# Values' stage of a one-core diffusion backbone: own buffers for the modulations' weights, TensorE's order by hand, fillers

## The chip, the cores and the metric

The kernel runs on one core of a Trainium2 chip. The metric is the time of one execution on the device in microseconds (us), from the first instruction to the last; lower is better. The kernel before took 1047.04 us, the median of 3 runs (1046.14 to 1047.27).

## The reference, cut to what matters

Two token groups go through two layers: 128 prompt tokens and 256 sample tokens, model width 1024. Each layer is a token mixer and a gated feed-forward, each after an RMSNorm and a modulation. What the change touches is the beginning of layer 0:

```python
sm, cm, gm, sf, cf, gf = adaln(c_ctx or c, w_ada[l], b_ada[l])  # silu(cond) @ w_ada + b_ada, split in 6
h = rmsnorm(x, g) * (1 + cm) + sm
q, k, v = qkv_proj(h, w_qkv)                # 1024 -> 3 * 1024
mix = attention(q, k, v) @ w_attn_out       # 16 heads of 64, with a position bias from rpb
```

So the values, v = h @ w_v, need h, and h needs 1/rms of every token and the shift sm and scale cm of every feature. Those come from a product of the two conditioning vectors (one for the prompt, one for the samples) with the first 2048 columns of w_ada.

## The kernel before, in words

Activations lie with features on partitions: x is eight tiles of 128 features by 384 tokens. All products are in float32 made of two parts: every operand is split into a high and a low part (hi and lo), and a product is three matmuls (hi by hi, hi by lo, lo by hi; the helper `mac`, L102 to L105). ScalarE (ACT) makes the high part of a weight tile (L96), VectorE (DVE) the low part (L97); `load` (L88) does both for a unit of 4 KB per partition, from a staging pool `stg` of three buffers into pools of five.

The values' stage, in the first lines of `attention` (L396 to L418), goes like this. `square` makes the squares of x, on ScalarE, and VectorE adds them up (L266 to L271); TensorE (PE) sums them over the partitions (`sums`, L280). `ada_block(0)` makes shift and scale of feature tile 0: 16 matmuls with 32-column stationary tiles (L145), ScalarE copies the result to SBUF (`ada_sb`, L149), TensorE transposes it (L151), and three small VectorE instructions (L154, L157, L117) finish the modulations `mod`. Then 1/rms is spread over the partitions by three matmuls (L294) and ScalarE copies it to SBUF (`R`, L404). For each feature tile k of eight: `modulated` makes h (VectorE's `t` L320, ScalarE's `hhi` L322, VectorE's `hlo` L324); the weights w_v of tile k are loaded; `ada_block(k + 1)` is written; and 18 matmuls of 512 columns add tile k's share to six PSUM banks (three token blocks by two halves of the features). At the end ScalarE copies the six banks to `V` (L417).

Then come, per pair of heads, `keys` and `queries` (24 matmuls each from a unit of w_qk, L103 to L105; their splits `ks` L440 and L441, `qd` and `ql` L453 to L455), `bias` (four DMAs into the one buffer `btr`, L471, and one VectorE instruction that writes `bt`, L477) and `scores` (L462 and L463, then VectorE's maxima L500 that read `bt`).

Two things set the order. A framework places each engine's instructions in one fixed order when the kernel is built, by priorities and its own estimate, except where `tc.keep_in_program_order` pins them; each engine then works through its list in that order. And a buffer of a pool is written again only when its last reader is done: `adp`, with ADA_BUFS = 4 buffers, holds the weights of two `ada_block`s (two tiles each, 512 KB a tile), which SyncE's queue (SP) issues in line with all other loads. `ps_ad`, with one PSUM bank, takes the sums of one `ada_block`.

Of the kernel before, what the change touches and what calls it, by code (L numbers as in the profile page):

```python
# [8 lines left out]
F32 = mybir.dt.float32  # L9
# [23 lines left out]
# columns of the packed per-feature parameters  # L33
# [6 lines left out]
def backbone(ctx: ExitStack, tc: tile.TileContext, xT_in, cond_in, condr_in, b_ada_in, prm_in,  # L40
# [21 lines left out]
    cond = cst.tile([P, KD, 2], F32, name="cond")  # L62
    nc.gpsimd.dma_start(cond, cond_in)
    x = [cst.tile([P, NT], F32, name=f"x{k}") for k in range(KD)]
    for k in range(KD):
        nc.sync.dma_start(x[k], xT_in[:, k, :])
# [10 lines left out]
    # TensorE runs at half its clock until it has been busy for a while  # L77
# [23 lines left out]
    def mac(out, a, b, start, stop):  # L101
        """out (+)= a.T @ b, both as (hi, lo)"""  # L102
        nc.tensor.matmul(out, a[0], b[0], start=start, stop=False)  # L103
        nc.tensor.matmul(out, a[0], b[1], start=False, stop=False)  # L104
        nc.tensor.matmul(out, a[1], b[0], start=False, stop=stop)  # L105
# [16 lines left out]
    def ada_load(f):  # L122
        w = []
        for hf in range(2):
            st = adp.tile([P, D], F32, name="adw", tag="adw")
# [4 lines left out]
    w_first = ada_load(0)  # L130
# [5 lines left out]
    def ada_block(f, tpool=ps_tb):  # L136
# [3 lines left out]
        w = ada_load(f) if f else w_first  # L140
        for kk in range(4):
            for hf in range(2):
                for q in range(2):
                    j = 2 * hf + q
                    nc.tensor.matmul(pa[32 * j:32 * j + 32, 0:P], cond_s[:, 4 * hf + kk, :],  # L145
                                     w[hf][:, kk, P * q:P * q + P], start=(kk == 0),
                                     stop=(kk == 3), tile_position=(0, 32 * j))
# [12 lines left out]
    class Ada:  # L160
        """pieces of 1024 modulations on TensorE, one unit (a feature tile of the conditioning)
        at a time; units are loaded ahead of their products"""
# [35 lines left out]
        def flush(self):  # L198
            """[32j + conditioning, 256 columns] to features on partitions"""
# [18 lines left out]
    class AdaV:  # L218
        """modulations on VectorE, 128 at a time"""
# [55 lines left out]
    def sums(pin=False):  # L275
        """every token's sum of squares"""
# [9 lines left out]
    def rms(ss=None, pin=False):  # L286
        """1/rms of every token, on all partitions: [P, NT] in PSUM"""
# [12 lines left out]
    def rsqrt(src, v, scale):  # L300
        """(src * scale + EPS) ** -0.5, refined by one Newton step"""
# [11 lines left out]
    # the modulated input of a layer's first products; its last two columns are the shifts  # L313
# [26 lines left out]
    def norm_first(nxt, units):  # L340
        """the first tiles' products as the tiles of x come, then h; returns the banks and R"""
# [13 lines left out]
    def late(ps, R, wkp):  # L355
        """products with 1/rms, and the shifts' products to add to them"""
# [23 lines left out]
    def attention(pool, wkp):  # L380
        # 0 where key column cc is in the window of query column c, else NEG
# [10 lines left out]
        V = pool.tile([P, 3, D], F32, name="V")  # L392
# [3 lines left out]

        # V, all its tiles at once, as the tiles of h come
        for k in range(KD):
            square(k, ("t384", "t384", "R0")[k % 3])
        ss = sums(True)  # L400
        ada_block(0, ps_ta)
        Rp = rms(ss, True)
        R = tmp.tile([P, NT], F32, name="R0", tag="R0")
        nc.scalar.copy(R, Rp[:, :NT])  # L404
        acc = [bank(q) for q in (ps_mm, ps_mm, ps_mm, ps_sc, ps_sc, ps_ta)]
        for k in range(KD):
# [391 lines left out]
```

## Time and profile before

| what | value |
|---|---|
| runs | 1047.27, 1047.04, 1046.14 us |
| span of the profiled execution | 1046.2 us |
| TensorE busy | 1027.7 us, 98% of the span |
| VectorE, ScalarE, GpSimd busy | 796.9, 496.8, 13.3 us |
| DMA | 174.32 MB, mean 167 GB/s |
| TensorE busy, 0 to 20 us | 13.91 us, granted clock 0.81 |
| TensorE busy, 20 to 66 us | 46.00 us, granted clock 0.97 |

The profile is of one execution, 0.8 us under the median of the runs. A row of the timeline reads: start, duration, engine, line, operation, what it writes and reads, count, and in brackets how long the engine stood before it and what released it. fp32 matmuls show as two records each. PEld is TensorE's loading of stationary tiles. In the rows of windows the columns are the stretch, its length, then busy time (and records) of the engines, the granted clock of TensorE, the DMA engines' busy share, and GB/s.

### The profile page before, as it was taken

What the parts mean: (1) busy time and instruction counts of PE and PEld (TensorE: products, weight loads), DVE (VectorE), ACT (ScalarE), POOL (GpSimd) and SP (SyncE); (2) the same over time, 40 slices, a digit from 0 to 9 for tenths busy, and PEclk for the clock granted to TensorE, in tenths of its full rate; (3) what the DMA queues carried; (4) which work ended last, traced back from release to release, by engine and by line L of the source; (5) the groups of instructions that cost most, each with busy time, mean ns of one, the idle gap of its engine ahead of it and who ended that gap; (6) DMA issues with size and microseconds to landing.
All of it is one profiled execution on the core that took longest, in us unless ns stands there. A gap on an engine that the chain in (4) does not pass through costs nothing.

```text
span 1046.2 us, 16013 instructions
## 1 busy us (share of the span) xinstructions
PE 1027.7 (98%) x5964; PEld 959.3 (92%) x5964; DVE 796.9 (76%) x1697; ACT 496.8 (47%) x862; POOL 13.3 (1%) x27
## 2 busy tenths in 40 slices
PE   7999999999999999999999999999999999999996
PEld 6787777679999999999998889999999999999995
DVE  3557666628899898999989979888599777777653
ACT  3357566536765544433346344444375544453330
POOL 1000000000000000000000000000000000000000
PEclk8999999999999999999999999999999999999998
DMA  7867666515255454566665765665414434435521
GB/s 274 310 191 208 187 186 194 192 61 171 81 153 181 161 156 150 161 199 211 217 196 174 247 205 157 198 191 195 144 65 157 142 122 123 134 109 169 163 69 61
DMA packets 64717, 174.32 MB, mean 167 GB/s; under 512 B 18800, under 2 KB 24064, under 8 KB 64640
## 3 DMA queue, kind: packets, MB, share of 16 engines
q1 hardware_dynamic: 63632, 171.46, 52.1%
q8 instruction: 47, 0.77, 0.3%
q0 software_dynamic: 432, 1.06, 0.3%
q10 hardware_dynamic: 576, 0.79, 0.2%
q14 instruction: 30, 0.25, 0.1%
HBM read 170.66 MB, written 2.62 MB: 166 GB/s over the span
## 4 chain that ended last, share of the span: by engine, by line
PE 92%; DMA 3%; DVE 2%; ACT 1%; SPq 1%; issue 1%; POOL 0%; POOLq 0%; DVEq 0%
PE bank L103 27%; PE bank L105 27%; PE bank L104 27%; DMA btr<-in_rpb 2%; PE bank L535 2%; PE bank L463 1%; PE bank L462 1%; PE bank L687 1%; PE bank L190 1%; PE bank L145 1%; PE bank L524 1%; DMA adw<-in_w_ada 1%; PE bank L532 1%; SPq L471 1%; PE bank L294 1%
## 5 line engine op out<-in xcount | busy, mean ns | idle before, releaser
L96 ACT CAST hi<-st 128x1024 fp32r<-128x1024 f32 (+1 forms) x216 | 222.5, 1032 | 315.3 <-PE bank L104 260.3
L105 PE MATMUL bank<-hhi,lo 128*128 128x384 f32 (+1 forms) x960 | 325.6, 339 | 0.4 <-DVE lo L97 0.4
L103 PE MATMUL bank<-hhi,hi 128*128 128x384 f32 (+1 forms) x960 | 325.7, 339 | 0.0
L104 PE MATMUL bank<-hlo,hi 128*128 128x384 f32 (+1 forms) x960 | 325.1, 339 | 0.0
L97 DVE TENSOR_TENSOR lo<-st,hi 128x1024 fp32r<-128x1024 f32 (+1 forms) x216 | 259.7, 1203 | 80.7 <-ACT hi L96 80.3
L103 PEld LDWEIGHTS bank<-hhi,hi 128*128 128x128 f32 x960 | 181.2, 189 | 3.5 <-issue 3.0
L105 PEld LDWEIGHTS bank<-hhi,lo 128*128 128x128 f32 x960 | 181.2, 189 | 1.3 <-DVE lo L97 0.7
L104 PEld LDWEIGHTS bank<-hlo,hi 128*128 128x128 f32 x960 | 180.6, 188 | 0.1
L248 DVE CUSTOM_DVE_ANT_0 junk<-adw,cs 128x1024 bf16<-128x1024 f32 x112 | 136.7, 1220 | 1.0
L105 PE MATMUL bank<-ahi,lo 128*128 128x384 f32 x352 | 119.0, 338 | 0.0
L104 PE MATMUL bank<-alo,hi 128*128 128x384 f32 x352 | 119.0, 338 | 0.0
L103 PE MATMUL bank<-ahi,hi 128*128 128x384 f32 x352 | 118.8, 338 | 0.0
L105 PEld LDWEIGHTS bank<-ahi,lo 128*128 128x128 f32 x352 | 66.1, 188 | 0.0
L104 PEld LDWEIGHTS bank<-alo,hi 128*128 128x128 f32 x352 | 66.1, 188 | 0.0
L103 PEld LDWEIGHTS bank<-ahi,hi 128*128 128x128 f32 x352 | 66.1, 188 | 0.0
L103 PE MATMUL bank<-hi,hhi 128*128 128x512 f32 x144 | 58.3, 409 | 1.8 <-ACT hhi L322 1.8
L105 PE MATMUL bank<-hi,hlo 128*128 128x512 f32 x144 | 57.5, 399 | 0.0
L104 PE MATMUL bank<-lo,hhi 128*128 128x512 f32 x144 | 57.4, 399 | 0.0
L368 DVE SCALAR_TENSOR_TENSOR x<-bank,mod,x 128x128 f32<-128x128 f32 x64 | 23.9, 413 | 37.6 <-PE bank L105 37.6
L103 PE MATMUL bank<-mhi,hi 128*128 128x384 f32 x128 | 43.4, 339 | 0.0
L105 PE MATMUL bank<-mhi,lo 128*128 128x384 f32 x128 | 43.2, 338 | 0.0
L104 PE MATMUL bank<-mlo,hi 128*128 128x384 f32 x128 | 43.1, 337 | 0.0
(151 smaller groups left out, 1288.7 us busy)
## 6 DMA issues: line engine op xcount, KB each, us to landing
st<-in_w_up SPq DMA_DIRECT2D x88, 512.0 KB, 3.5
adw<-in_w_adaT SPq DMA_DIRECT2D x56, 512.0 KB, 3.6
adw<-in_w_ada SPq DMA_DIRECT2D x40, 512.0 KB, 5.8
st<-in_w_down SPq DMA_DIRECT2D x32, 512.0 KB, 3.6
st<-in_w_qk SPq DMA_DIRECT2D x16, 512.0 KB, 6.7
st<-in_w_gu SPq DMA_DIRECT2D x16, 512.0 KB, 4.2
st<-in_w_gv SPq DMA_DIRECT2D x16, 512.0 KB, 4.3
st<-in_w_gout SPq DMA_DIRECT2D x16, 512.0 KB, 4.2
```

Of the source, the lines that this page charges most:

```text
L96: nc.scalar.copy(hi[:, :n], st[:, :n])
L97: nc.vector.tensor_tensor(lo[:, :n], st[:, :n], hi[:, :n].bitcast(F32), ALU.subtract)
L103: nc.tensor.matmul(out, a[0], b[0], start=start, stop=False)
L104: nc.tensor.matmul(out, a[0], b[1], start=False, stop=False)
L105: nc.tensor.matmul(out, a[1], b[0], start=False, stop=stop)
L145: nc.tensor.matmul(pa[32 * j:32 * j + 32, 0:P], cond_s[:, 4 * hf + kk, :], w[hf][:, kk, P * q:P * q + P], start=(kk == 0), stop=(kk == 3), ...
L190: nc.tensor.matmul(self.pa[32 * j:32 * j + 32, 0:256], cond_s[:, k, :], t[:, 256 * j:256 * j + 256], start=(k == 0), stop=(k == KD - 1), t ...
L248: tc.keep_in_program_order(nc.vector.tensor_tensor_reduce(self.junk, t, self.cs[c], 1.0, 0.0, ALU.mult, ALU.add, m[:, c:c + 1]))
L294: mm = nc.tensor.matmul(R[:, b * P:(b + 1) * P], r[:, b:b + 1].to_broadcast([P, P]), ident, start=True, stop=True)
L368: nc.vector.scalar_tensor_tensor(x[m][:, a:b], ps[:, a:b], mod(l, gate, m, c), x[m][:, a:b], ALU.mult, ALU.add)
L462: nc.tensor.matmul(out, qd[hh][:, qs], ks[hh][:, cs], start=True, stop=False)
L535: nc.tensor.matmul(pv[hs, NPR:NT], vv, pT[:, 256 * i:256 * i + 256], start=(i == 0), stop=(i == 2), tile_position=(0, 64 * hh))
```

## The change

Beside comments, it does the following.

- x is loaded in four DMAs of two tiles each, where there were eight.
- The values' stage is a function of its own, `project_values`, and V lies in a pool `v` around it. Inside, a pool `vw` of six buffers takes the weights of `ada_block(1)` to `ada_block(7)`; `ada_block(0)` still uses `adp`. The attention's pools `att` and `attw` are opened after `vw` is closed, so their first tiles (the mask, `cv`, the attention's results) lie where `vw` was.
- The loads for blocks 1 and 2 are issued right after w_v's first tile; those for block k + 3 in step k, after w_v's tile k + 1.
- The 16 matmuls of each `ada_block` and the values' matmuls are pinned in the order they are written: 18 matmuls of tile k, by part (six hi by hi, six with h's low part, six with w's low part), then `ada_block(k + 2)`; after tile 0, blocks 1 and 2. The transposes are not pinned.
- Fillers: five matmuls of 128 columns after the sums of squares, and six after those that spread 1/rms.
- Tile 0's `t` reads 1/rms from PSUM; the copy to SBUF serves the other tiles.

```diff
+    xp = [cst.tile([P, 2, NT], F32, name=f"x{k}") for k in range(0, KD, 2)]
+    x = [xp[k // 2][:, k % 2, :] for k in range(KD)]
+    for k in range(KD // 2):
+        nc.sync.dma_start(xp[k], xT_in[:, 2 * k:2 * k + 2, :])
...
+    def project_values(V, vp):
...
+        def keep_warm(src, n):
+            warm = bank(ps_ad)
+            for _ in range(n):
+                tc.keep_in_program_order(
+                    nc.tensor.matmul(warm[:, :P], src[:, :P], ones, start=True, stop=True))
+
+        aw = {0: w_first}
+        ws = {0: load(w_v[0])}
+        for f in (1, 2):
+            aw[f] = ada_load(f, vp)
+        for k in range(KD):
+            square(k, ("t384", "t384", "R0")[k % 3])
+        ss = sums(True)
+        keep_warm(sq["last"], 5)
+        ada_block(0, aw.pop(0), ps_ta)
+        Rp = rms(ss, True)
+        keep_warm(ones, 6)
...
+        for k in range(KD):
+            modulated(0, SM, CM, k, R if k else Rp)
+            if k == 0:
+                nc.scalar.copy(R, Rp[:, :NT])
+            if k + 1 < KD:
+                ws[k + 1] = load(w_v[k + 1])
+            if k + 3 < KD:
+                aw[k + 3] = ada_load(k + 3, vp)
+            w = ws.pop(k)
+            for part, (ih, iw) in enumerate(((0, 0), (1, 0), (0, 1))):
+                for half in range(2):
+                    for b in range(3):
+                        tc.keep_in_program_order(nc.tensor.matmul(
+                            acc[3 * half + b], h(k, slice(b * P, (b + 1) * P))[ih],
+                            w[iw][:, half, :], start=(k == 0 and part == 0),
+                            stop=(k == KD - 1 and part == 2)))
+            for f in (k + 2,) if k else (1, 2):
+                if f in aw:
+                    ada_block(f, aw.pop(f))
...
-        for k in range(KD):
-            modulated(0, SM, CM, k, R)
-            w = load(w_v[k])
-            if k < KD - 1:
-                ada_block(k + 1)
-            for half in range(2):
-                for b in range(3):
-                    mac(acc[3 * half + b], h(k, slice(b * P, (b + 1) * P)),
-                        wsel(w, half, slice(0, 512)), k == 0, k == KD - 1)
```

What this does to the built order shows in three places. First TensorE, in the middle of the stage, where one `ada_block` (`adw`) and its transpose (`ada_sb`) stand among the values' matmuls (`hhi` and `hlo` are h, `hi` and `lo` the weights). Before:

```order
L105 MATMUL bank<-hi,hlo 128x512
L145 MATMUL bank<-adw,cond_s 32x128 x16
L103 MATMUL bank<-hi,hhi 128x512
L104 MATMUL bank<-lo,hhi 128x512
L105 MATMUL bank<-hi,hlo 128x512
L151 MATMUL bank<-ident,ada_sb 128x128
L103 MATMUL bank<-hi,hhi 128x512
```

And now, the same place:

```order
L415 MATMUL bank<-lo,hhi 128x512 x6
L146 MATMUL bank<-adw,cond_s 32x128 x16
L152 MATMUL bank<-ident,ada_sb 128x128
L415 MATMUL bank<-hi,hhi 128x512 x6
L415 MATMUL bank<-hi,hlo 128x512 x6
```

The transpose stood two to six values' matmuls behind the block whose result it takes; now it follows it directly, with ScalarE's copy between the two.

Second VectorE, at the passage from the last tile of h (`hlo`) to the first scores; `bt` is a pair's bias, `ks` and `ql` the low parts of keys and queries, the ISA rows the scores' maxima. Before:

```order
L324 SCALAR_TENSOR_TENSOR hlo<-t_680,mod_143,hhi 128x256
L97 TENSOR_TENSOR lo<-st,hi 128x1024 x2
L477 TENSOR_TENSOR bt<-btr,mask 128x768
L97 TENSOR_TENSOR lo<-st,hi 128x1024 x2
L441 TENSOR_TENSOR ks<-kT,ks 64x512 x2
L477 TENSOR_TENSOR bt<-btr,mask 128x768
L455 SCALAR_TENSOR_TENSOR ql<-bank,qd 64x384
L500 ISA bank,st<-bank,bt 128x256
```

And now:

```order
L325 SCALAR_TENSOR_TENSOR hlo<-t_660,mod_135,hhi 128x256
L500 TENSOR_TENSOR bt<-btr,mask 128x768
L98 TENSOR_TENSOR lo<-st,hi 128x1024 x2
L500 TENSOR_TENSOR bt<-btr,mask 128x768
L464 TENSOR_TENSOR ks<-kT,ks 64x512 x2
L478 SCALAR_TENSOR_TENSOR ql<-bank,qd 64x384 x2
L523 ISA bank,st<-bank,bt 128x256
```

The bias of the second pair moved from behind the first keys' low parts to ahead of them.

Third SyncE's queue, at the end of the stage. Before:

```order
L93 DMA st<-in_w_v 128x1024
L420 DMA cv<-in_cv 128x1024
L430 DMA kT<-in_ckT 128x128
L93 DMA st<-in_w_qk 128x1024 x2
L471 DMA btr<-in_rpb 64x6x64 x4
L430 DMA kT<-in_ckT 128x128
```

And now:

```order
L94 DMA st<-in_w_v 128x1024 x2
L453 DMA kT<-in_ckT 128x128
L94 DMA st<-in_w_qk 128x1024
L494 DMA btr<-in_rpb 64x6x64
L94 DMA st<-in_w_qk 128x1024
L494 DMA btr<-in_rpb 64x6x64 x2
L443 DMA cv<-in_cv 128x1024
L494 DMA btr<-in_rpb 64x6x64
L453 DMA kT<-in_ckT 128x128
L94 DMA st<-in_w_qk 128x1024 x2
```

`cv` moved behind three of the four bias loads, and it waits for the last matmuls of `ada_block(7)`, whose buffers it lies in.

More of the change, by code (lines that the diff above doesn't have):

```diff
@@ L63, in backbone @@
     nc.gpsimd.dma_start(cond, cond_in)
-    x = [cst.tile([P, NT], F32, name=f"x{k}") for k in range(KD)]
-    for k in range(KD):
-        nc.sync.dma_start(x[k], xT_in[:, k, :])
+    xp = [cst.tile([P, 2, NT], F32, name=f"x{k}") for k in range(0, KD, 2)]
+    x = [xp[k // 2][:, k % 2, :] for k in range(KD)]
+    for k in range(KD // 2):
+        nc.sync.dma_start(xp[k], xT_in[:, 2 * k:2 * k + 2, :])
     zero = cst.tile([P, 1], F32, name="zero")
@@ L120, in gain, with ada_load @@
             ALU.add, ALU.mult)
-    def ada_load(f):
+    def ada_load(f, pool):
         w = []
         for hf in range(2):
-            st = adp.tile([P, D], F32, name="adw", tag="adw")
+            st = pool.tile([P, D], F32, name="adw", tag="adw")
             w.append(st.rearrange("p (a b) -> p a b", b=256))
@@ L144, in ada_block @@
                     j = 2 * hf + q
-                    nc.tensor.matmul(pa[32 * j:32 * j + 32, 0:P], cond_s[:, 4 * hf + kk, :],
-                                     w[hf][:, kk, P * q:P * q + P], start=(kk == 0),
-                                     stop=(kk == 3), tile_position=(0, 32 * j))
+                    tc.keep_in_program_order(
+                        nc.tensor.matmul(pa[32 * j:32 * j + 32, 0:P], cond_s[:, 4 * hf + kk, :],
+                                         w[hf][:, kk, P * q:P * q + P], start=(kk == 0),
+                                         stop=(kk == 3), tile_position=(0, 32 * j)))
         sb = tmp.tile([P, 256], F32, name="ada_sb", tag="ada_sb")
@@ L377, in wsel, with attention @@
         return w[0][:, k, s], w[1][:, k, s]
-    def attention(pool, wkp):
+    def project_values(V, vp):
+        def keep_warm(src, n):
+            warm = bank(ps_ad)
+            for _ in range(n):
+                tc.keep_in_program_order(
+                    nc.tensor.matmul(warm[:, :P], src[:, :P], ones, start=True, stop=True))
[10 more added lines that the diff above has]
+        keep_warm(ones, 6)
+        R = tmp.tile([P, NT], F32, name="R0", tag="R0")
+        acc = [bank(q) for q in (ps_mm, ps_mm, ps_mm, ps_sc, ps_sc, ps_ta)]
+        for k in range(KD):
[17 more added lines that the diff above has]
+                    ada_block(f, aw.pop(f))
+        for b in range(3):
+            for half in range(2):
+                nc.scalar.copy(V[:, b, 512 * half:512 * half + 512], acc[3 * half + b])
+        nc.gpsimd.dma_start(sv_out, V[:, 0, :])
+    def attention(V, pool, wkp):
         mask = pool.tile([P, 64], F32, name="mask")
@@ L395, in attention @@
         olo = [pool.tile([P, NT], F32R, name=f"olo{t}") for t in range(NPAIR)]
[L398 to L406, printed above, removed]
-            modulated(0, SM, CM, k, R)
-            w = load(w_v[k])
-            if k < KD - 1:
-                ada_block(k + 1)
-            for half in range(2):
-                for b in range(3):
-                    mac(acc[3 * half + b], h(k, slice(b * P, (b + 1) * P)),
-                        wsel(w, half, slice(0, 512)), k == 0, k == KD - 1)
-        for b in range(3):
-            for half in range(2):
-                nc.scalar.copy(V[:, b, 512 * half:512 * half + 512], acc[3 * half + b])
-        nc.gpsimd.dma_start(sv_out, V[:, 0, :])
         nc.sync.dma_start(cv, cv_in)
@@ L710, in gmlp @@
             residual(1, GM, m, ps, (1, SF, CF))
-    with tc.tile_pool(name="att", bufs=1) as pool, tc.tile_pool(name="attw", bufs=2) as wkp:
-        attention(pool, wkp)
+    with tc.tile_pool(name="v", bufs=1) as vpool:
+        V = vpool.tile([P, 3, D], F32, name="V")
+        with tc.tile_pool(name="vw", bufs=6) as wkp:
+            project_values(V, wkp)
+        with tc.tile_pool(name="att", bufs=1) as pool, tc.tile_pool(name="attw", bufs=2) as wkp:
+            attention(V, pool, wkp)
     csp = ctx.enter_context(tc.tile_pool(name="cs", bufs=1))
```

6 lines of the change are left out of this document (2 added, 4 removed).

## Prediction, made before the change was run

> **What bounds the kernel now.** I read the page first, then who TensorE waits for, then the timeline of the first 80 us.
>
> ```profile
> span 1046.2 us, 16013 instructions
> ...
> PE   7999999999999999999999999999999999999996
> ```
> ```profile
> PE bank L294 <- DVE rr L310: 1.9, 1, 1.9
> PE bank L103 <- ACT hhi L322: 1.8, 1, 1.8
> PE bank L280 <- DVE sqacc L271: 1.8, 1, 1.8
> ...
> PE bank L145 <- DMA adw<-in_w_ada: 0.7, 1, 0.7
> ```
>
> TensorE is busy from the first slices to the last: whatever delays it by 1 us anywhere makes the kernel 1 us longer. Only the first slice has room. And the modulations' weights (`adw`), which now get six buffers, hold TensorE up once, 0.7 us, for the block that keeps its old buffers. So loading ahead brings nothing by itself; the order does whatever is done. The stage to be costed ends where the first keys begin:
>
> ```profile
> 3.27 0.52 ACT L266 ACTIVATE sqacc<-x 128x384 f32<-128x384 f32 x1 [1.03 <-DMA x<-in_xT]
> 4.91 0.22 ACT L72 ACTIVATE cond_s<-cond 128x16 f32<-128x16 f32 x1 [1.12 <-DMA cond<-in_cond]
> 5.57 3.88 DVE L271 TENSOR_TENSOR sqacc<-sqacc,t 128x384 f32<-128x384 f32 x6 [4.25 <-ACT t L269]
> 9.50 0.83 PE L280 MATMUL bank<-ones,sqacc 128*128 128x2 f32 x6 [1.78 <-DVE sqacc L271]
> 10.93 0.41 PE L145 MATMUL bank<-adw,cond_s 128*32 128x128 f32 x4
> 12.03 1.45 PE L145 MATMUL bank<-adw,cond_s 128*32 128x128 f32 x28 [0.68 <-DMA adw<-in_w_ada]
> 13.93 0.45 PE L151 MATMUL bank<-ident,ada_sb 128*128 128x128 f32 x1 [0.45 <-ACT ada_sb L149]
> 14.16 1.50 PE L294 MATMUL bank<-ident,rr 128*128 128x128 f32 x6
> 16.08 1.05 ACT L96 CAST hi<-st 128x1024 fp32r<-128x1024 f32 x1
> 16.22 0.75 DVE L320 SCALAR_TENSOR_TENSOR t<-x,mod,R 128x128 f32<-128x128 f32 x2 [1.26 <-ACT R L404]
> 17.03 0.80 ACT L322 ACTIVATE hhi<-t,mod 128x128 fp32r<-128x128 f32 x2
> 17.48 1.22 PE L103 MATMUL bank<-hi,hhi 128*128 128x512 f32 x2 [1.81 <-ACT hhi L322]
> 31.73 0.39 PE L105 MATMUL bank<-hi,hlo 128*128 128x512 f32 x1
> 63.72 0.39 PE L104 MATMUL bank<-lo,hhi 128*128 128x512 f32 x1
> 63.95 0.40 PE L105 MATMUL bank<-hi,hlo 128*128 128x512 f32 x1
> 64.19 0.34 PE L103 MATMUL bank<-hhi,hi 128*128 128x384 f32 x1
> ```
>
> Values' products run from 17.48 to 64.19. The last two start 0.23 apart: the pitch of one product at full clock. The 36 of tiles 0 and 1, with modulation blocks 1 and 2, are through at 31.73 + 0.23 = 31.96.
>
> **The clock at the start.** Granted clock (the figure before the DMA share), and the warm-up's own records (L80 alone, first two rows):
>
> ```profile
> 6.50:7.00 0.50, 0.50 (x7) 0.50 (x6) 1.00 0.99 260
> 7.50:8.00 0.50, 0.22 (x2) 0.03 (x1) 1.00 1.00 252
> 12.00:12.50 0.50, 0.47 (x19) 0.48 (x22) 0.20 (x2) 0.00 (x0) 0.43 (x3) 1.00 1.00 410
> 12.50:13.00 0.50, 0.50 (x18) 0.48 (x10) 0.31 (x2) 0.00 (x0) 0.24 (x1) 0.56 1.00 410
> 22.50:23.00 0.50, 0.50 (x18) 0.47 (x8) 0.00 (x0) 0.00 (x0) 0.00 (x0) 0.70 0.00 0
> ```
>
> The last wide matmul of the warm-up ends at 7.72; the clock falls to half just after 12.5 and comes back at about 22.8. Between lie only the two-column sums and the 32-column block.
>
> **Part by part.**
>
> *x in pairs, and ScalarE's order.* Four issues fewer bring the weights earlier, but another chain is later: `cond_s` now stands ahead of the squares on ScalarE, and it starts at 4.91. The first square moves from 3.27 to 5.13, VectorE's first addition to 5.13 + 2 x 0.52 = 6.2, its six additions (3.88) end at 10.1, where TensorE's sums started at 9.50: 0.6 later. The sums took 10.93 - 9.50 = 1.43, so they end at 11.55.
>
> *First fillers, block 0.* Seven records in 0.5 us and two records a matmul give 0.14 each: five take 0.7, to 12.25. The weights landed at about 12.0 before and are not later now. If the clock is held, the block takes about 1.1, to 13.35; ScalarE's copy and the transpose follow as before 0.45 later, at 13.8; the three matmuls of 1/rms take half of 1.50, to 14.8. The six fillers (0.85) end at 15.65, under the wait for h.
>
> *Tile 0.* `t` reads PSUM and no longer waits for the copy `R`: it starts at 14.85, its first group takes some 0.28 of the 0.75 for both, `hhi`'s first some 0.35 of 0.80, to 15.5. But ScalarE's list has the 1.05 of the weights' cast between the two groups of `hhi`: 16.6, then the second group to 17.0. TensorE makes one product at 16.6 and the other 17, of 0.23 each, from 17.0: tile 0 ends at 21.0.
>
> *Middle of the stage.* These rows give the period:
>
> ```profile
> 37.76 0.40 PE L105 MATMUL bank<-hi,hlo 128*128 128x512 f32 x1
> 39.09 0.51 PE L103 MATMUL bank<-hi,hhi 128*128 128x512 f32 x1
> 39.31 0.27 ACT L149 COPY ada_sb<-bank 128x128 f32<-128x128 f32 x1 [2.50 <-PE bank L145]
> 39.67 0.29 PE L151 MATMUL bank<-ident,ada_sb 128*128 128x128 f32 x1
> 43.27 0.40 PE L105 MATMUL bank<-hi,hlo 128*128 128x512 f32 x1
> ```
>
> A tile with a block takes 43.27 - 37.76 = 5.51: 1.1 for the block (37.99 to 39.09), 4.4 for 18 products and the transpose. The transpose can't start before 39.67, since the copy ends at 39.58; before, values' products filled the 39.09 to 39.67. Now nothing stands between, so TensorE waits 0.58 at the most, and 0 if the copy came at once; nothing shortens the copy, so I take 0.5 a tile, a little off the top for the restart that the products behind the block paid anyway.
>
> Between tiles 0 and 1 stand two blocks with two such waits, and `hhi` of tile 1 behind the second copy on ScalarE, its second group 0.5 after the transpose: 1.2 + 0.6 + 1.2 + 0.6 + 0.5 = 4.1. With 4.2 for the products, tile 1 ends at 29.3, 2.65 before 31.96. Five periods of 5.51 + 0.5 and a last tile of 4.15 make 34.2: the stage ends at 63.5 instead of 64.19. Gain so far 0.7. That is the whole of it: blocks placed behind whole tiles win 2.65 at the start, and the transposes give 2.5 back (0 if something hid them, 2.9 by the full 0.58).
>
> *Passage to the attention.* The rows of before:
>
> ```profile
> 61.64 0.95 DVE L477 TENSOR_TENSOR bt<-btr,mask 128x768 f32<-128x768 f32 x1
> 71.31 1.41 DVE L441 TENSOR_TENSOR ks<-kT,ks 64x512 fp32r<-64x512 f32 x2
> 73.83 0.63 PE L462 MATMUL bank<-ks,qd 128*128 128x384 f32 x2
> 74.35 0.96 DVE L477 TENSOR_TENSOR bt<-btr,mask 128x768 f32<-128x768 f32 x1 [1.63 <-DMA btr<-in_rpb]
> 75.82 0.44 PE L463 MATMUL bank<-ks,ql 64*128 64x384 f32 x1 [0.50 <-DVE ql L455]
> ```
> ```profile
> DMA to landing us min/median/max: 4.3/6.9/9.8
> ```
>
> The last row is for the bias loads. Now `cv` waits for block 7, two tiles and a transpose's wait before the end, 8.9 before it; SyncE's next issue is the last bias load of pair 0, 8.4 to 7.8 before the end. By the shortest landing, 4.3 (three of four have landed, one load is ahead), `bt` of pair 0 runs 3.5 to 2.5 before the end; before, it ended 1.6 before. From its end to the start of pair 1's `bt` it was 74.35 - 62.59 = 11.76, since the one buffer must be reloaded. So pair 1's `bt` runs from 9.2 to 10.2 after the end of the stage, and `ks`, now queued behind it, has its first half done at 10.9. The scores stood 73.83 - 64.19 = 9.64 after the end. They come 1.3 later; TensorE has keys and queries until about then (9.64 before), and then waits. The old wait of 0.5 for `ql` and three keys' products that fall behind the scores are nearly paid back by `ql` following 0.55 after `ks`: 1.2 net.
>
> The six copies of V come later, too: all banks end in the last six products. ScalarE has pair 1's keys' cast (1.05) ahead of them, whose load is issued 7.5 before the end; by landings of 4.3 to 6.9 it costs the first keys 0 to 1: I take 0.4.
>
> *The rest* keeps its work. The order of attention is shuffled in places, and TensorE is as full there as the page's slices show: 0, between -1 and 1.
>
> Sum: -0.7 + 1.2 + 0.4 = +0.9. The profiled execution (1046.2) would become 1047.1; against the runs' median, 0.84 above it, that is 1047.9, with 1046.6 to 1049.2 by the ends of the small terms.
>
> **The rivals.** About 0.2%, 2.1 us, is what a measurement of this kernel can tell from no change: below 1044.9 is faster, above 1049.1 slower.
>
> A, slower: the clock falls before tile 0, as it did. It decides by whether 0.7 us of fillers at 11.55 count. Block 0 then takes 0.35 longer, the transpose and 1/rms matmuls 0.75, tile 0 starts at 17.7 and pays 0.2 more a product until the clock is back: at 19.4 (the last change less one third of the 10.2 between the two changes, an estimate) tile 0 ends 1.7 later, at 22.8 3.2 later: 1049.6 to 1051.1. For it: the same span of weak work from 7.72. Against: the fillers are wide.
>
> [...]
>
> B, slower: the last bias load lands by the median 6.9 instead of 4.3. Every later step of `bt`, `ks` and scores shifts by 2.6: 1050.5. For it: `cv`, 512 KB, goes ahead of it in the same queue. It decides from landings above 6.
>
> C, faster: the 2.65 stays. If the transposes cost 0.1 instead of 0.5 and pair 1's bias lands before the keys are through (below 7 after the end), the sum is -0.7 - 2.0 = -2.7: 1044.3. Against: both are fixed orders.
>
> D: the change does not do what it says, since nothing waited for the buffers: gains and waits cancel within 0.5, 1047.0.
>
> **How the numbers follow.** My forecast 0.38; A 0.24; B 0.12; C 0.17; D 0.09. Forecast and D lie within 0.2% but for 0.03 of the forecast's top: 0.44. Slower: A, B and that 0.03, 0.39. Faster: C, 0.17. Forecast and D alone span 1046.5 to 1049.2. For eight in ten the range goes down to 1044.7, which leaves out most of C, and up to 1051.0, where the ends of A and B stay out.
>
> **What would show it.** Right: sums at 10.1; tile 0's second product near 17.0 at granted clock 1.00; seven more transposes with some 0.5 of wait each for `ada_sb`; first keys near 63.5; first scores 11 after them, waiting for `ks`. Wrong: clock 0.5 after 12.5 (A); transposes without a wait, or scores 9.6 after the keys (C); first keys later than 65.

## The result, and the profile after

The changed kernel takes 1060.07 us, the median of 4 runs (1059.31 to 1063.03), against 1047.15 for the kernel before in the same session: a ratio of 1.0124, with a 95% interval of 1.0110 to 1.0138. It is slower by 12.9 us, and outside the predicted range. The profiled execution has a span of 1058.5 us, 12.3 more than before; those 12.3 are what is accounted for here.

The page of the changed kernel, the span and TensorE's slices (26.5 us each) with the granted clock:

```profile
span 1058.5 us, 16052 instructions
...
PE   8989999999999999999999999999999999999996
...
PEclk8998999999999999999999999999999999999998
```

One slice more than before isn't full, the third (53 to 79 us), and the clock is down in the fourth (79 to 106) as well as in the first. From there on the span is as full as it was. Whom TensorE waits for in the changed kernel (total, times, longest):

```profile
PE bank L152 <- ACT ada_sb L150: 3.7, 8, 0.5
PE bank L281 <- DVE sqacc L272: 1.9, 1, 1.9
...
PE bank L485 <- ACT pr L507: 1.6, 1, 1.6
PE bank L104 <- ACT V L424: 1.5, 1, 1.5
...
PE bank L485 <- DVE ks L464: 1.1, 1, 1.1
```

Seven of the eight waits for `ada_sb` are the predicted ones; the eighth, block 0's, is in the kernel before too. The three below are at the passage to the attention: first keys (`V`), first scores (`ks`), second head's scores (`pr`). TensorE's timeline shows where each stands:

```profile
10.43 1.16 PE L281 MATMUL bank<-ones,sqacc 128*128 128x2 f32 x6 [1.94 <-DVE sqacc L272]
12.73 2.48 PE L388 MATMUL bank<-ones,t 128*128 128x128 f32 x10
15.27 1.94 PE L146 MATMUL bank<-adw,cond_s 128*32 128x128 f32 x32
20.46 1.84 PE L415 MATMUL bank<-hi,hhi 128*128 128x512 f32 x6 [0.47 <-ACT hi L97]
33.27 1.08 PE L146 MATMUL bank<-adw,cond_s 128*32 128x128 f32 x32
39.26 1.08 PE L146 MATMUL bank<-adw,cond_s 128*32 128x128 f32 x32
45.24 1.08 PE L146 MATMUL bank<-adw,cond_s 128*32 128x128 f32 x32
65.86 1.56 PE L415 MATMUL bank<-lo,hhi 128*128 128x512 f32 x6
68.93 0.44 PE L104 MATMUL bank<-hhi,hi 128*128 128x384 f32 x1 [1.50 <-ACT V L424]
79.74 0.59 PE L485 MATMUL bank<-ks,qd 128*128 128x384 f32 x2 [1.06 <-DVE ks L464]
90.23 0.44 PE L485 MATMUL bank<-ks,qd 128*128 128x384 f32 x1 [1.63 <-ACT pr L507]
```

So the lag behind the kernel before grows in steps:

| place on TensorE | before | after | lag |
|---|---|---|---|
| tile 0's first product | 17.48 | 20.46 | 3.0 |
| tile 1 through | 31.96 | 33.3 | 1.3 |
| last product of the values | 64.35 | 67.42 | 3.1 |
| first keys | 64.19 | 68.93 | 4.7 |
| first scores | 73.83 | 79.74 | 5.9 |
| second head's scores | 81.42 | 90.23 | 8.8 |
| third head's scores | 88.12 | 98.57 | 10.5 |
| last values of pair 7 | 230.04 | 242.14 | 12.1 |

The last values' product is taken at its end (start and duration). A quarter of the loss comes in the stage that was changed, and three fifths within 35 us behind it. ScalarE's timeline there:

```profile
67.35 1.04 ACT L97 CAST hi<-st 128x1024 fp32r<-128x1024 f32 x1 [5.81 <-DMA st<-in_w_qk]
68.30 3.02 ACT L424 COPY V<-bank 128x512 f32<-128x512 f32 x6
...
86.58 1.05 ACT L97 CAST hi<-st 128x1024 fp32r<-128x1024 f32 x1 [4.67 <-DMA st<-in_w_qk]
87.65 1.28 ACT L507 ACT_TABLE_LOAD   x1
88.95 0.58 ACT L507 ACTIVATE pr<-bank,st 128x384 f32<-128x384 f32 x1
```

In these rows the list is worked through in its order: the cast of pair 1's key weights stands ahead of the copies of V, and it waited for its load until 67.35; the cast of pair 2's stands ahead of the first exponentials, and it waited until 86.58, though the maxima were ready at about 84. In the kernel before, the same piece of ScalarE's list has the table load and the exponentials first and the cast behind them:

```profile
78.84 1.28 ACT L484 ACT_TABLE_LOAD   x1 [2.06 <-DVE st L505]
80.14 0.58 ACT L484 ACTIVATE pr<-bank,st 128x384 f32<-128x384 f32 x1
...
81.97 1.06 ACT L96 CAST hi<-st 128x1024 fp32r<-128x1024 f32 x1
```

And two of the three waits at the passage were paid twice, for the granted clock fell to 0.50 behind them: behind the 1.1 us for `ks` and behind the 1.6 us for `pr`. Behind the 1.5 us for `V` it stayed at full (1.00 from 66 to 80). Windows of the changed kernel (the granted clock is the figure before the DMA share):

```profile
82.00:82.50 0.50, 0.50 (x3) 0.45 (x3) 0.50 (x1) 0.00 (x0) 0.00 (x0) 0.95 0.10 41
83.00:84.00 1.00, 1.00 (x5) 1.00 (x4) 0.89 (x6) 0.00 (x0) 0.00 (x0) 0.50 0.58 106
85.50:86.00 0.50, 0.50 (x4) 0.50 (x3) 0.00 (x0) 0.00 (x0) 0.00 (x0) 0.64 0.63 82
92.50:93.00 0.50, 0.50 (x4) 0.50 (x4) 0.47 (x2) 0.00 (x0) 0.00 (x0) 0.69 0.77 272
96.00:96.50 0.50, 0.50 (x9) 0.17 (x11) 0.00 (x0) 0.50 (x2) 0.00 (x0) 0.90 0.52 197
```

By the shares of these windows the clock is at half from 82.45 to 85.86 and from 92.69 to 96.10: 1.7 us of work lost each time (3.41 x 0.5), as much as the wait ahead of it or more. In the sum from 64 to 100: 1.5 and 1.1 and 1.6 of waits and 3.4 by the clock are 7.6, against a growth of the lag of 7.4 (from 3.1 to 10.5).

### The profile page after: what moved, and what is told of

Read it like the earlier page. It is cut to its first block, busy times and chain, and to the rows that moved or that the text cites. A ratio compares the mean times of both kernels' runs of the same rounds, so it can differ in the third digit from the quotient of the medians.

```text
span 1058.5 us, 16052 instructions
## 1 busy us (share of the span) xinstructions
PE 1034.0 (98%) x5986; PEld 966.2 (91%) x5986; DVE 797.0 (75%) x1697; ACT 495.9 (47%) x862; POOL 14.4 (1%) x27
## 3 DMA queue, kind: packets, MB, share of 16 engines
q0 software_dynamic: 432, 1.06, 0.3%
## 4 chain that ended last, share of the span: by engine, by line
PE 91%; DMA 3%; DVE 2%; ACT 2%; issue 0%; SPq 0%; POOL 0%; POOLq 0%; DVEq 0%; ACTq 0%
PE bank L104 27%; PE bank L105 26%; PE bank L106 26%; DMA st<-in_w_qk 2%; PE bank L558 2%; PE bank L415 2%; PE bank L486 1%; PE bank L485 1%; PE bank L710 1%; PE bank L191 1%; DMA out_skT<-kT 1%; PE bank L146 1%; PE bank L547 1%; PE bank L281 1%; ACT hi L97 1%; PE bank L555 1%
## 5 line engine op out<-in xcount | busy, mean ns | idle before, releaser
L323 ACT ACTIVATE hhi<-t,mod 128x128 fp32r<-128x128 f32 x64 | 26.9, 452 | 26.3 <-DVE t L321 17.2
L105 PE MATMUL bank<-lo,hhi 128*128 128x512 f32 x96 | 37.9, 394 | 0.0
L104 PE MATMUL bank<-hi,hhi 128*128 128x512 f32 x96 | 37.8, 394 | 0.0
```

Source lines behind the costliest of these rows:

```text
L323: nc.scalar.activation(hhi[:, k, a:b], u[:, a:b], AF.Identity, bias=mod(l, shift, k, c))
```

## The experiments

What the waits come from is the question: they could be the cause, or only the form in which something else shows. Three theories at first. **S**: ScalarE's list is at fault, with casts ahead of the copies of V and of the exponentials. **Q**: SyncE's queue is, because `cv` lies in the six buffers' memory and holds everything behind it until block 7. **T**: the values' stage is, and the rest only follows. For comparison each run has its ratio to the kernel before (the changed kernel's is 1.0124) and TensorE's loss from 66 to 100 us: 34 less its busy time, and of the busy time the part that the granted clock took away. What is lost behind 100 us isn't in it: in e1, e5, e11 and e17 the clock was down for some us more there (granted 0.96, 0.87, 0.96 and 0.93 from 100 to 140). For the kernel before, the changed one, and the four parts run alone, that row of the windows, one fence each, in the order before, after, start alone (e13), order alone (e14), fillers alone (e16):

```profile
66.00:100.00 34.00, 33.09 (x182) 27.52 (x181) 24.20 (x70) 19.39 (x42) 1.61 (x3) 1.00 0.69 193
```
```profile
66.00:100.00 34.00, 29.24 (x147) 24.50 (x145) 17.04 (x42) 18.44 (x36) 1.69 (x3) 0.90 0.61 172
```
```profile
66.00:100.00 34.00, 33.51 (x185) 28.07 (x184) 23.84 (x69) 20.03 (x43) 1.62 (x3) 1.00 0.69 194
```
```profile
66.00:100.00 34.00, 29.01 (x150) 24.17 (x149) 19.13 (x54) 16.90 (x35) 1.08 (x2) 0.90 0.63 185
```
```profile
66.00:100.00 34.00, 33.98 (x205) 27.70 (x203) 24.63 (x75) 21.40 (x48) 1.62 (x3) 1.00 0.70 192
```

Before: 34 - 33.09 = 0.9. After: 4.76 and 29.24 x 0.10 = 2.92, together 7.7. All runs:

| run | median | ratio (95%) | loss 66 to 100 | TensorE's largest wait there |
|---|---|---|---|---|
| e1_castlate | 1063.5 | 1.0137 (1.0111 to 1.0163) | 12.0 | 4.0 for `ql`, 3.8 for `adw` |
| e2_ownmask | 1058.9 | 1.0100 (1.0084 to 1.0115) | 7.1 | 4.0 for `pr` |
| e3_tlate | 1055.6 | 1.0067 (1.0051 to 1.0084) | 7.5 | 4.6 for `ql` |
| e4_nopin | 1054.3 | 1.0057 (1.0042 to 1.0072) | 7.7 | 4.8 for `ql` |
| e5_own_cast | 1063.1 | 1.0142 (1.0116 to 1.0167) | 6.6 | 3.8 for `ql` |
| e6_nopin_own | 1052.7 | 1.0060 (1.0034 to 1.0086) | 7.4 | 4.4 for `ql` |
| e7_nofill | 1060.5 | 1.0123 (1.0100 to 1.0145) | 8.8 | 3.3 for `pr` |
| e8_b_six | 1056.3 | 1.0082 (1.0062 to 1.0102) | 6.4 | 3.3 for `ql` |
| e9_a_bias | 1055.9 | 1.0079 (1.0060 to 1.0099) | 6.0 | 3.5 for `pr` |
| e10_nopin_bias | 1056.0 | 1.0083 (1.0066 to 1.0100) | 5.9 | 3.1 for `pr` |
| e11_b_bias | 1056.9 | 1.0086 (1.0068 to 1.0104) | 2.6 | 2.1 for `qd` (to 100.5) |
| e12_best | 1059.5 | 1.0112 (1.0090 to 1.0133) | 8.2 | 5.3 for `adw` |
| e13_b_start | 1047.2 | 0.9995 (0.9986 to 1.0005) | 0.5 | 0.5 for `ql` |
| e14_b_order | 1057.7 | 1.0107 (1.0081 to 1.0132) | 7.9 | 5.0 for `pr` |
| e15_b_six_own | 1054.6 | 1.0072 (1.0055 to 1.0089) | 6.0 | 2.2 for `ql` |
| e16_b_fill | 1045.6 | 0.9990 (0.9981 to 0.9999) | 0.0 | none |
| e17_a_swap | 1064.9 | 1.0171 (1.0157 to 1.0185) | 8.6 | 4.7 for `pc` |
| e18_bo_swap | 1055.7 | 1.0078 (1.0065 to 1.0090) | 4.2 | 1.0 for `pr` |

### Taking one cause away from the changed kernel

**e1_castlate**, the casts placed later:

```diff
+        pre[1, 0] = load(w_qk[1, 0]); pre[0, 0] = load(w_qk[0, 0])
         (copies of V)
+        pre[1, 1] = load(w_qk[1, 1], pin=True)
...
             nc.scalar.copy(kT[:, 0:NT], pk[:, :NT])
+            if t == 1:
+                pre[1, 2] = load(w_qk[1, 2], pin=True)
```

> Kernel after, with the casts of the keys' and queries' weights placed later in ScalarE's list: pair 0's stay ahead of the copies of V, pair 1's keys' cast stands behind them, and pair 2's keys' cast behind the copy of pair 1's keys, so behind the first exponentials' table load. The context values' load still stands in SyncE's queue behind block 7. Theory S (the loss is ScalarE's fixed list: casts that wait for late loads ahead of the copies of V and of the first exponentials): first keys within 4 us of the stage's last product's place in kernel after (65.5 to 67.5 instead of 68.9), second head's scores without the 1.6 wait, total about 1052 to 1054. Theory T (the loss is made in the values' stage, by the half clock at the start and the transposes' waits, and the rest only follows): nothing after 64 matters, 1059 or more. Theory Q (SyncE's queue stands still until block 7, and whatever order ScalarE has, the loads come too late): 1058 to 1060, with the waits moved from ScalarE to TensorE.

Measured 1063.5. The copies of V did get their place (keys at 67.84 instead of 68.93), and no exponential waits. But pair 0's bias ran at 68.60 and pair 1's at 81.02 (66.05 and 77.92 in the changed kernel), VectorE's `ql` behind it, and TensorE waited 4.0 for that and 3.8 for a modulation's weights. S alone falls.

**e2_ownmask**, `mask` and `cv` beside V, out of the weight buffers' memory:

```diff
         V = vpool.tile([P, 3, D], F32, name="V")
+        mask = vpool.tile([P, 64], F32, name="mask")
+        cv = vpool.tile([P, D], F32, name="cv")
```

> Kernel after, with the mask and the context values' tile in memory of their own instead of memory that the six weight buffers leave, so that SyncE's queue isn't held until block 7; ScalarE's list of casts stays about as in kernel after. Theory Q: the keys' weights land before their casts are due, waits of ScalarE for them fall from 15.1 us in the first 220 us to about 3, total 1051 to 1053. Theory S (the place of the casts in ScalarE's list decides): about 1057. Theory T: 1059, as kernel after.

Measured 1058.9. The bias came at 62.78 and 74.94, about as early as in the kernel before (61.64 and 74.35), and the first scores 2.7 sooner than in the changed kernel; then the exponentials waited behind pair 2's cast and TensorE for them, 4.0. Q alone falls: its wait was real, and another took its place.

**e3_tlate**, the transposes of blocks 2 to 7 behind the next tile's first six products:

```diff
             for part, (ih, iw) in enumerate(((0, 0), (1, 0), (0, 1))):
+                if part == 1 and todo is not None:
+                    ada_end(*todo)
```

> Kernel after, with the transposes of blocks 2 to 7 moved behind the first six products of the next tile, so that values' products cover ScalarE's copy of the block. By itself that takes away 6 waits of 0.5 us; as a side effect the copies of V come ahead of pair 1's casts again in ScalarE's list and the exponentials' table load ahead of pair 2's cast. Theory T (the waits of the transposes are the loss, the rest follows): the period falls from 5.98 to about 5.5 and the total by 3 or less, 1057. Theory S (the casts' places): 1050, with the first scores' waits gone.

Measured 1055.6, between the two. First keys came at 64.75 instead of 68.93; of those 4.2 all were gone again at the second head's scores but for 1.4 (88.80 against 90.23), since TensorE waited 4.6 for `ql`, which stood behind pair 1's bias (78.47).

**e4_nopin**, the products and the blocks no longer pinned:

```diff
-                        tc.keep_in_program_order(nc.tensor.matmul(acc[3 * half + b], ...))
+                        nc.tensor.matmul(acc[3 * half + b], ...)
```

> Kernel after, with TensorE's fixed order in the values' stage taken away (the products and the blocks); the six buffers, the loads ahead, the fillers, the loads of x in pairs and the early conditioning stay. The copies of V come ahead of pair 1's casts again. Theory S with T: the fixed order is what costs, 1049 to 1051, the remainder being the slow clock at the start. Theory Q: SyncE is held until block 7 in this kernel as well, so 1056 or more.

Measured 1054.3. The stage was 1.3 ahead of the kernel before at the first keys (62.92), though tile 0 began 1.4 later; all of it and 5.3 more went at the second head's scores (86.75). VectorE shows it:

```profile
69.42 1.40 DVE L463 TENSOR_TENSOR ks<-kT,ks 64x512 fp32r<-64x512 f32 x2
76.83 0.96 DVE L499 TENSOR_TENSOR bt<-btr,mask 128x768 f32<-128x768 f32 x1 [6.00 <-DMA btr<-in_rpb]
77.70 0.54 DVE L477 SCALAR_TENSOR_TENSOR ql<-bank,qd 64x384 fp32r<-64x384 f32 x1
```

The keys' low parts are done at 70.8 and the queries stand ready from about 72.5, and VectorE waits 6.0 for pair 1's bias that stands ahead of it.

**e7_nofill**, the changed kernel without its eleven fillers:

```diff
-        keep_warm(sq["last"], 5)
-        keep_warm(ones, 6)
```

> Kernel after without its eleven fillers, else the same. Theory F (at the start the first five fillers only stand ahead of block 0 at half clock, 2.4 us, and keep no clock): tile 0's first product comes about 2.4 us sooner, near 18, and the total falls by 2 to 3, to 1057 to 1058. Theory K (they keep the clock from being lower for longer): the half clock lasts as long or longer, tile 0 ends no sooner, 1060 or more.

Measured 1060.5 (ratio 1.0123 against 1.0124). F is right for the start and K for the total: tile 0's first product came 2.0 sooner (18.44), but its six took 2.92 instead of 1.84 since the half clock lasted longer (to 21.3 instead of 17.6), and at the first keys 1.2 were left (67.69), which the later waits swallowed.

### Taking two or three away

**e5_own_cast** (e1 and e2 together) and **e6_nopin_own** (e4 with e2's memory) test whether two chains hide each other:

> Both edits of the first two runs in one kernel: the mask and the context values in memory of their own, and the casts of the keys' weights placed later. Alone, the late casts changed the total from 1060.1 to 1063.5 and the memory of its own to 1058.9, since after each another wait was the last one. Theory W (two chains end at the first scores and softmaxes, and each hides the other: the bias of pair 1 on VectorE, late because its loads stand behind the context values' in SyncE's queue; and pair 2's keys' cast ahead of the exponentials on ScalarE): with both gone the first scores come within 10.5 us of the first keys and the second head's scores wait for no exponential, 1051 to 1054, the remainder being the values' stage. Theory T (the values' stage decides, the rest follows): 1058 or more.

> The kernel without the fixed order (1054.3), with the mask and the context values in memory of their own. Theory W: its one large wait, 4.8 us of TensorE for pair 0's low parts of the queries, stands behind pair 1's bias on VectorE, and that behind the bias's loads, and those behind the context values' load that waits for block 7; it shrinks below 1 us and the total falls to 1049 to 1051. Against W (the bias is late from the single bias buffer alone, whatever SyncE's queue does): the wait stays over 4, 1054.

Measured 1063.1 and 1052.7. W falls: in e5 pair 1's bias still came at 80.24, `ql` cost 3.8, and from 100 to 140 TensorE lost 7.5 more (idle and clock), with 2.6 of waits for `qd`; in e6 the wait stayed at 4.4, with the bias at 76.65. So the bias is not late from `cv` alone.

**e9_a_bias**, **e10_nopin_bias** and **e11_b_bias** move the loads and the additions of the first two biases into the stage, in the changed kernel, in e4's and in the kernel before:

```diff
             w = ws.pop(k)
+            if k in (3, 5):
+                bts.append(bias(len(bts)))
```

> Kernel after with the biases of pairs 0 and 1 loaded and masked during the values' stage (at tiles 3 and 5), into memory of their own beside V, with the mask and the context values there too. Theory B (the first scores' time is set by pair 1's bias, which VectorE has ahead of pair 0's keys or queries: it came 12.2 us after pair 0's in all nine kernels, through the one buffer, and pair 0's is late by its loads): the first scores come within 9.7 us of the first keys' place, and the total falls by the waits there and the half clock that they bring, 3 to 6 us: 1054 to 1057; what is left is the values' stage and ScalarE's casts. Theory T (values' stage alone): 1059 or more.

> The kernel without the fixed order (1054.3), with the biases of pairs 0 and 1 in the values' stage as in the run before. Theory B: its wait of 4.8 us for the queries' low parts, which had pair 1's bias ahead of them, goes, and with it the half clock behind it (2 x 1.7 us at the most): 1047 to 1050. Against B (something else holds the scores, the bias only happens to come last): another wait of 3 us or more stands in its place, 1052 to 1054.

> Kernel before with nothing but the biases of pairs 0 and 1 moved into the values' stage. Theory B: kernel before has 0.5 us of wait there, pair 1's bias comes just when it is needed, so at most 0.5 to 1 is to be had: 1046 to 1047. If the bias's loads in the stage hold up the weights of the values: 1048 or more.

Measured 1055.9, 1056.0 and 1056.9. The wait behind pair 1's bias (for `ks` in the changed kernel, for `ql` in e4) was gone in the first two; in its place TensorE waited 3.5 and 3.1 for `pr`, behind weights' casts that waited for their loads. In the third the stage into which the loads were put became late itself: the first keys came at 73.14 instead of 64.19, with 2.9 of waits for `hhi` that the kernel before doesn't have, and the clock fell twice (at about 46 and 63; granted 0.89 from 34 to 50, 0.90 from 50 to 66); which load held it up is not shown. B is right for the wait and wrong for the time.

**e12_best** puts late casts, late transposes and early biases together:

> Kernel after with three edits: biases of pairs 0 and 1 in the values' stage, casts of the keys' weights placed later on ScalarE, transposes of blocks 2 to 7 behind the next tile's first six products. Theory B with S and T added up: no wait over 1 us after the values' stage, and that stage ends at about 64.5, as in kernel before: 1046 to 1049. If the waits only change places again: 1054 or more.

Measured 1059.5: first keys at 67.88, then 5.3 for a modulation's weights. The waits changed places once more.

### One part of the change at a time, in the kernel before

This settled most. The diffs show only what matters, with loops drawn together. **e8_b_six** is the six buffers and the loads ahead, **e15_b_six_own** the same with `mask` and `cv` elsewhere, **e14_b_order** the fixed order (with the four old buffers), **e13_b_start** the paired loads of x and the fillers, **e16_b_fill** the fillers alone.

```diff
 e8:  +            for f in range(1 if k == 0 else k + 3, min(k + 4, KD)):
      +                aw[f] = ada_load(f, vp)
 e14: +                        tc.keep_in_program_order(nc.tensor.matmul(acc[3 * half + b], ...))
      +            for f in (k + 2,) if k else (1, 2): ada_block(f, aw.pop(f))
 e16: +        keep_warm(sq["last"], 5)
               ada_block(0, ps_ta)
               Rp = rms(ss, True)
      +        keep_warm(ones, 6)
```

> Kernel before with one part of the change alone: the six buffers of the modulations' weights in memory that attention takes over afterwards, loaded ahead; no fillers, order as the scheduler makes it, start as before. Theory W: the context values' load waits for block 7 in SyncE's queue, the bias of pair 0 and with it that of pair 1 come 3 to 5 us later, and TensorE waits for scores: 1050 to 1052. If the buffers cost nothing: 1047.

> Kernel before with the new start alone: x loaded in pairs and the eleven fillers; no other buffers, TensorE's order in the values' stage as the scheduler makes it. ScalarE's and VectorE's lists from the copies of V on stand in kernel before's order. Theory L (lists: what costs is the place of casts, biases and copies in the lists, not lateness): only the start's own delay is seen, 1 to 3 us at tile 0, and no wait over 1 us between keys and pair 2: 1047 to 1050. Theory D (lateness: attention's loads arrive just in time and any shift opens waits): waits of 3 us or more there, 1053 or more.

> Kernel before with TensorE's order alone: values' products part by part and blocks behind whole tiles, fixed; old start, no fillers, the four old buffers for the blocks' weights, each loaded a tile or two ahead as far as these reach. ScalarE's list then has pair 1's keys' cast ahead of the copies of V and pair 2's ahead of the exponentials, VectorE's has pair 1's bias ahead of the keys, as in kernel after. Theory L: the waits of kernel after come with these lists, 1054 to 1058. Theory D: the stage ends no later than before, so nothing is late: 1046 to 1049.

> Kernel before with the six buffers loaded ahead (1056.3 alone), and with the mask and the context values in memory of their own, so that no load of attention waits for block 7. If the memory that attention takes over is what the buffers cost: 1047 to 1050. If it is the loads ahead, which come before the values' weights in SyncE's queue and hold up the first tiles: 1053 to 1056, with the first keys as late as in the run with the buffers alone (67.9).

> Kernel before with the eleven fillers alone. The first five stand ahead of block 0, whose weights land at 12.0: 0.7 us at full clock, 2.4 at half. If they keep the clock at full: tile 0 starts sooner than 17.5 or as soon, 1045.5 to 1047.5. If not: 1.0 to 2.5 us later, 1048 to 1050.

- **The start costs nothing** (0.9995). Its first product of tile 0 is at 20.51, as late as the changed kernel's, and the first keys at 64.89, 0.7 late; then the largest wait is 0.5, as in the kernel before, and the lag is gone at the end. A lateness of 0.7 opens no waits. That speaks against theory D, but doesn't show what a lateness of 3 us, as in the changed kernel, would do with the old lists.
- **The order alone costs 1.07%**, close to the 1.24% of the whole change. Its keys come at 64.32 and its first scores at 73.98, 0.15 behind the kernel before. (Luck has a part in that: in this execution the clock held until 17.0 and tile 0 began at 15.85, 1.6 early, which paid for the transposes' waits.) Then ScalarE and TensorE, with one row of each:

```profile
82.33 1.04 ACT L96 CAST hi<-st 128x1024 fp32r<-128x1024 f32 x1 [6.66 <-DMA st<-in_w_qk]
83.40 1.28 ACT L492 ACT_TABLE_LOAD   x1
```
```profile
85.98 0.69 PE L470 MATMUL bank<-ks,qd 128*128 128x384 f32 x1 [4.98 <-ACT pr L492]
```

  That is 5.0 of wait and 2.9 by the clock, in the one place where pair 2's cast stands ahead of the exponentials. The load isn't to blame: the kernel before casts the same weights at 81.97, hardly sooner than 82.33, but behind its exponentials (the rows above). That is L: the list, with next to nothing late.
- **The buffers alone cost 0.82%**, and 0.72% with the memory elsewhere. Most of it is the loads ahead, not the memory: pair 1's bias comes at 80.29 and at 78.43, against 74.35 before, the first keys 3.7 and 2.9 late, the second case of e15's expectation. In the stage itself both have the same four waits that the kernel before doesn't have, 2.5 us in all: for the copies of two blocks one right behind the other (0.5 and 1.1, at about 28 to 31), then for w_v's `hi` and `lo` (0.6 and 0.3, to 34). In e8 0.8 of a later start come on top.
- The parts together (1.07% and 0.82%) would be 1.9%; the change is 1.24%. They don't add; both lose in the same passage, so one may hide the other.
- **The fillers alone** give 0.9990 (0.9981 to 0.9999), the fastest kernel here, by 1.0 to 1.7 us and just clear of no change; the first keys came at 62.62 in its profiled execution.

### Mending the load instead of the list

**e17_a_swap** and **e18_bo_swap** swap two lines in `keys`, so that a pair's weights are issued ahead of its cached keys; TensorE's, ScalarE's and VectorE's lists stay as they are in e17.

```diff
-            nc.sync.dma_start(kT[:, NT:512], ckT_in[:, t, :])
             w = load(w_qk[1, t])
+            nc.sync.dma_start(kT[:, NT:512], ckT_in[:, t, :])
```

> Kernel after with two lines of the keys swapped: SyncE issues a pair's key weights ahead of its cached keys, instead of behind them. The cached keys of pair 2 wait for a buffer until 81.97, and pair 2's weights stood behind them (82.34). TensorE's, ScalarE's and VectorE's lists stay as they are. Theory L (ScalarE's list with the early cast, and the load that it waits for, are the cause of the second half of the loss): the weights are issued near 73, the cast waits no more, the exponentials run 4 us sooner; the 1.6 us of wait, the half clock at 82.4 to 85.8 (1.7) and perhaps that at 92.6 to 96 (1.7) go, and the total falls by 3 to 5: 1055 to 1057. Pair 1's cast ahead of the copies of V and the bias keep their 2.6 us. Against L: 1059 or more.

> The kernel before with TensorE's new order alone (1057.7), with the same two lines swapped. Its stage ends as early as before's, and its one large wait is 5.0 us for the exponentials, behind pair 2's keys' cast, whose load was issued at 78.11; with 3.4 us lost to the half clock from 80 to 100. Theory L: the load is issued near 68, both go, 8.4 us: 1048 to 1051. If something else makes the scores late: another wait of 3 us or more, 1054 or more.

Measured 1064.9 and 1055.7. Both totals lie on the side that the expectations set against L. e17 is slower than the changed kernel (1.0171 against 1.0124), and e18 gains about 3 us on e14 by the ratios, where 7 to 10 were expected. The traces show what was right and what was missing.

In e17 the load was issued at 72.32 instead of 82.34, but it landed about 11 us after that, where it had taken 4.2, so the cast ran at 83.30 instead of 86.58. It still waited 2.4 for it. The second head's scores came at 86.95 instead of 90.23, just the 3.28 by which the cast was sooner. The third head's came at 98.13 instead of 98.57: the next cast in ScalarE's list, ahead of the next exponentials, waited 6.1 for its own load until 95.03, about as late as in the changed kernel (95.46), and TensorE 4.7 for that. Behind this wait the clock was at half from 98.4 to 105.2, 3.4 us of work, of which the table has only the first part.

In e18 the large wait shrank from 5.0 to 1.0 and the loss from 7.9 to 4.2. Pair 1's cast waited 4.3 for its load, and the copies of V stood behind it, but TensorE didn't wait for them. That the first keys came 2.1 later (66.42) is the start of this execution: the clock fell at about 11.7 and came back at about 21.9 (granted 0.79 in the first 20 us), and tile 0 began 2.2 later than in e14's.

So a waiting cast sets the time at its place in the list, and an earlier load helps there alone: the list has several such places. L is right for the place, and wrong for what mending one load is worth.

## Why the prediction was wrong

- **"The rest": the step that failed.** It read "The order of attention is shuffled in places, and TensorE is as full there as the page's slices show: 0, between -1 and 1". It cost about 6 us: 2.9 at the second head's scores, 1.7 at the third's by the clock, 1.6 after. Full slices say that the old lists hid every load. They say nothing of new lists, and there casts and a bias had moved ahead of what TensorE waits for. Of the 11.4 us between the forecast and the profiled execution (12.3 against 0.9) this step makes 6.4; the end of the stage makes 3.8 and the passage up to the first scores 1.2.
- **"Loading ahead brings nothing by itself; the order does whatever is done."** The first half is wrong in sign: it costs 0.82% (e8). The second holds for most of it (e14), but by ScalarE's list and not by TensorE's transposes.
- **The start.** The squares' sums began at 10.43, forecast 10.1. Rival A came true, and earlier than it was priced: the clock fell at about 10.8, in the sums (0.77 granted from 10.5 to 11.0, 0.50 from 11.0), so tile 1 ended at 33.3, not 29.3. The five fillers took 2.5 us (12.73 to 15.27) instead of 0.7, and the clock made 1.1 of that difference; the rest is that 0.14 a filler was misread. The seven records of that window include those that reach over its ends; at full clock five fillers took 1.36 us in e16 (11.19 to 12.55). A's question, whether the fillers count, did not arise in the changed kernel. In e16 they ran at full clock, and it fell at 12.5 all the same. A's 19.4 for the end of the half clock was an estimate, and so was its chance of 0.24 against the forecast's 0.38: the half clock ended at 17.6, and no run shows what makes the clock fall. What the start cost in the changed kernel isn't shown: in the kernel before, the same start costs nothing in the end (e13).
- **The transposes.** Right: 3.7 us in eight waits, and a period of 45.24 - 39.26 = 5.98, forecast 6.01.
- **The end of the stage.** Forecast 63.5; 67.4 measured, the 4.0 by which tile 1 ended late.
- **The passage.** The mechanism was right and its size was not. VectorE's rows:

```profile
66.05 0.96 DVE L500 TENSOR_TENSOR bt<-btr,mask 128x768 f32<-128x768 f32 x1 [3.99 <-DMA btr<-in_rpb]
77.92 0.96 DVE L500 TENSOR_TENSOR bt<-btr,mask 128x768 f32<-128x768 f32 x1 [4.40 <-DMA btr<-in_rpb]
```

  Pair 1's bias began 10.9 after the end of pair 0's (forecast 11.76) and first scores waited for `ks` behind it. But pair 0's bias ran at 66.05, 1.4 before the end of the values and not 3.5 to 2.5 (rival B's late landing), and the copies of V behind pair 1's cast, taken at 0.4 with bounds of 0 and 1, cost 1.5.
- **Rivals C and D** have nothing for them. Not one of the rivals named pair 2's cast ahead of the exponentials, although it could be read in ScalarE's new order.
- **Doubled waits.** No term counted the half clock behind a wait. It made 3.4 of the 7.4 us by which the lag grew from the end of the stage to the third head's scores.

What stays open: how much of the changed kernel's loss is ScalarE's list and how much the later bias, since each hides the other; no run had the new order with the old lists of ScalarE and VectorE. Nor is it shown what made the scheduler put two blocks one behind the other in e8 and e15, where most of the stage's lateness of 2.9 to 3.7 arose.

## What to carry to other kernels

When a scheduler fixes each engine's list at build time, read the lists behind the changed stage, not only in it: look for an instruction that waits for a load, now ahead of one on which the critical engine waits. In a passage where loads land just in time, run each part of a change alone before anything is mended, since mending one wait showed only the next; and allow for a slower clock behind a wait of TensorE: here it came behind waits of 1.06 and 1.63 us (0.50 granted, for 3.41 us each) and not behind one of 1.50.

## What the runs showed of the hardware

- The granted clock changed in steps of 3.41 us: in the changed kernel at 82.45, 85.86, 92.69 and 96.10, of which the third lies three steps behind the first. The fall at 10.77 and the return at 17.59 lie two steps apart, and 82.45 lies nineteen behind that.
- Standing still was not all that decided. In the changed kernel the clock fell after steps in which TensorE stood still for only about 1.0 of 3.4 us (79.0 to 82.4 has 0.98, 89.3 to 92.7 has 0.95) and ran narrow score matmuls (64x384, 128x128 and 64x128) for a part of the rest. It stayed at full after the step from 65.4 to 68.8 (counted back from 82.45), with 1.4 of standing still (67.42 to 68.80) behind products of 512 columns. The 0.5 us wait at the first scores of the kernel before and of e13 left it at full too (1.00 from 66 to 100). What decides is not shown.
- The clock fell at the start in all twenty kernels, with the fillers or without (granted 0.76 to 0.92 in the first 20 us): at about 10.3 (e8) to 13.1 (e15), and in e14 at 17.0. How long it stayed at half differs. With the fillers it was one or two steps in twelve of thirteen kernels (12.5 to 15.9 in e16, 10.8 to 17.6 in the changed kernel) and three in e1; without them it was three or four in six of seven (12.5 to 22.8 in the kernel before), and one in e14. That is one profiled execution of each kernel.
